# First projections of a hybrid decoder layer in pairs by seven half-sized products, and two branches' gates moved beside the RWKV chain and kept in DRAM

## The chip, the cores and the metric

The kernel runs on one core of one Trainium2 chip. The metric is the device time of one execution in microseconds, as the median of several runs. An engine here is PE (TensorE, the matrix unit), DVE (VectorE), ACT (ScalarE), POOL (GpSimd) or SP (SyncE, which issues the DMAs). Each engine executes its own program in order, and waits for semaphores that the others raise.

## What is computed

One decoder layer on x of 1024 tokens by 1024 channels, in float32. The reference, cut to what the change touches:

```python
def reference(x, mem, w_in, ...):
    p = x @ w_in[l]
    (p_rw, p_cv, g_q, g_k, g_v, g_r, g_z,
     f_q, f_k, f_v, f_z, p_gate) = _split(p, COL_SIZES)
    u_rw = _rwkv7_branch(p_rw, ...) @ rw_up[l]
    u_cv = _conv_branch(p_cv, ...) @ cv_up[l]
    u_gla = _gla_branch(g_q, g_k, g_v, g_r, g_z, ...) @ gla_up[l]
    u_fox = _fox_branch(f_q, f_k, f_v, f_z, fox_bf[l]) @ fox_up[l]
    gates = jax.nn.sigmoid(p_gate.reshape(Bsz, T, N_BRANCH, D) + gate_b[l])
    merged = (gates[:, :, 0] * u_rw + gates[:, :, 1] * u_cv
              + gates[:, :, 2] * u_gla + gates[:, :, 3] * u_fox)
    x = _layer_norm(ALPHA * x + merged @ w_out[l], ln_g[l, 0], ln_b[l, 0])
    y = _cross_attention(x, mem, xa_wq[l], xa_wk[l], xa_wv[l], xa_wo[l])
    x = _layer_norm(ALPHA * x + y, ln_g[l, 1], ln_b[l, 1])
    y = _swiglu(x, ffn_w1[l], ffn_w3[l], ffn_w2[l])
    x = _layer_norm(ALPHA * x + y, ln_g[l, 2], ln_b[l, 2])
```

`p_rw` is the input of a recurrence over the tokens (RWKV-7), which is computed in chunks; FoX is a softmax attention with a decay.

## The kernel before

All data stands transposed: channels on the 128 partitions, tokens along the free axis, in two halves `hf` of 512 tokens. w_in is cut into 57 blocks of 128 output columns: 9 for RWKV (`RW_BLOCKS`; block 8, `misc`, holds small inputs), 16 for the convolution, GLA and FoX (`ST_BLOCKS`), and 32 for the gates, 8 for each of four branches. A float32 operand is split into a rounded high part (cast on ACT) and the remainder (subtraction on DVE, sometimes POOL), by `split`; `mm3` then makes a product of three matmuls: high by high, low weights by high, high by low. A block against one half of the tokens is 8 x 3 = 24 matmuls of 128x512, so a block is 48.

The order of the work is that in which Python generators are drained, and each engine's program follows it. At first x is loaded and split into `xh`, `xl` (16 tiles of 128x1024). Then the loop over `RW_BLOCKS` (L324) projects the 9 blocks one after the other: `project` makes the matmuls into a PSUM tile `ps_g`, ACT copies them into `praw`, and five DVE operations apply the token shift (L329 to L333). Weights come by `weight` (L166): a 512 KB load into `wraw`, `whi` by ACT, `wlo` by DVE.

Then follows the chain (`rwkv`), a long row of small dependent steps. `weave` takes one piece of filler matmuls between any two steps; its filler is `stage_projections`, the 16 `ST_BLOCKS` in pieces of six matmuls, stored to DRAM. The merge comes next: `gates(br, t2)` gives, for each branch, for each of 8 row blocks j and each half, 24 gate matmuls (`ps_gate`), a sigmoid on ACT (`gsig`, L1051) and six matmuls (`ps_up`) that project the branch's output y up; DVE multiplies the two (L1056) and POOL adds them to `merged[j]` (L1057). These pieces are the filler of GLA, the convolution and FoX; of FoX's steps each takes `FOX_PIECES` of them, and what is left over is drained behind it. Then come `ps_wo` (the output projection, which reads `merged` as `mA` and `mB`), cross attention and the FFN. The FFN already pairs its blocks: the product of a 2 x 2 arrangement of quarter blocks is done by seven products of half the contraction instead of eight (a Winograd form), with combinations of weights made by `comb` and `sums` on POOL.

The loop that is replaced:

```python
    for bi, n in enumerate(RW_BLOCKS):
        raw = pM.tile([P, T], F32, tag="M", name="praw")
        drain(project(io["wblk"][bi], lambda hf, ps: nc.scalar.copy(raw[:, hs(hf)], ps),
                      (w_first, w_second, None)[min(bi, 2)]))
```

## Time and profile before

| what | value |
|---|---|
| median of 3 runs | 2102.21 us (2099.38 to 2107.37) |
| profiled execution, its own time | 2108.64 us |
| its span (first to last instruction) | 2106.9 us |
| its mean granted TensorE clock | 0.986 |
| PE busy | 2071.2 us, 98% of the span |
| DVE, ACT, POOL busy | 56%, 36%, 16% |
| projections of RW blocks; chain with ST blocks | 7 to 107 us; 107 to 447 us |
| merge with GLA and convolution; with FoX; the rest of the gates | 447 to 571.8; 571.8 to 843.5; 843.5 to 1014.2 us |

The three runs come from executions without the profiler; the trace is one further execution, whose own time stands in the second row. A busy PE means that it has matmuls in flight: they are pipelined, so the rate is read from the number of matmuls in a stretch. A granted clock of 1.00 in a window is 2.4 GHz, 0.50 is 1.2 GHz.

### The profile page before, as it was taken

The page shows a single profiled execution, that of the slowest core. Times are in us where ns is not written, and L with a number is a line of the kernel's source. Part 1 is how long each engine was busy: PE and PEld are TensorE (multiplying, and loading weights), DVE is VectorE, ACT ScalarE, POOL GpSimd, SP SyncE. Part 2 cuts the span into 40 slices and gives each one's busy share as a digit, 9 for nine tenths or more (in the row PEclk, how much of TensorE's full clock was granted, in tenths as well). Part 3 has the DMA queues.
Part 4 walks back from the last instruction along what each step waited for, and adds up shares of the span by engine and source line. Part 5 has one row for each costly group of instructions (what it writes and reads, how often), then busy time and mean ns, then how long its engine had stood idle before and what let it go on. Part 6 is the DMA issues. An engine that isn't in the chain of part 4 may idle for free.

```text
span 2106.9 us, 28921 instructions
## 1 busy us (share of the span) xinstructions
PE 2071.2 (98%) x11524; PEld 1698.4 (81%) x11524; DVE 1189.7 (56%) x2097; ACT 768.7 (36%) x1287; POOL 342.3 (16%) x268
## 2 busy tenths in 40 slices
PE   9999999999999999999999999999999999999997
PEld 7877877787888888888888888877888888888877
DVE  5465398624534443233476345677666666666666
ACT  3243222157466565222234233443232222322321
POOL 0000000000001211121024000147131111222333
PEclk9999999999999999999999999999999999999998
DMA  6123231232211211111543102331211211211102
GB/s 218 51 65 87 68 100 60 74 103 84 89 47 53 66 61 38 56 50 43 165 146 125 45 31 80 109 102 40 100 40 43 78 41 41 70 51 51 66 24 80
DMA packets 86102, 154.83 MB, mean 73 GB/s; under 512 B 19430, under 2 KB 43800, under 8 KB 85968
## 3 DMA queue, kind: packets, MB, share of 16 engines
q1 hardware_dynamic: 85968, 152.99, 22.4%
q8 instruction: 91, 1.49, 0.3%
q14 instruction: 43, 0.35, 0.1%
HBM read 128.20 MB, written 24.76 MB: 73 GB/s over the span
## 4 chain that ended last, share of the span: by engine, by line
PE 91%; DVE 2%; POOL 2%; issue 2%; ACT 1%; DMA 1%; SPq 0%; DVEq 0%; POOLq 0%; ACTq 0%
PE ps_w L183 9%; PE ps_w L179 9%; PE ps_w L182 9%; PE ps_gate L179 6%; PE ps_gate L183 5%; PE ps_gate L182 5%; PE ps_g L179 5%; PE ps_g L183 4%; PE ps_g L182 4%; PE ps_q L182 3%; PE ps_q L183 3%; PE ps_q L179 2%; PE ps_up L179 1%; PE ps_up L182 1%; PE ps_up L183 1%
## 5 line engine op out<-in xcount | busy, mean ns | idle before, releaser
L183 PE MATMUL ps_gate<-xl,whi 128*128 128x512 f32 x512 | 201.6, 394 | 0.0
L182 PE MATMUL ps_gate<-xh,wlo 128*128 128x512 f32 x512 | 201.3, 393 | 0.0
L162 DVE TENSOR_TENSOR wlo<-wraw,whi 128x1024 fp32r<-128x1024 f32 x99 | 136.5, 1379 | 61.6 <-ACT whi L161 61.4
L179 PE MATMUL ps_gate<-xh,whi 128*128 128x512 f32 x512 | 165.6, 402 | 0.0
L182 PE MATMUL ps_g<-xh,wlo 128*128 128x512 f32 x400 | 158.3, 396 | 0.0
L183 PE MATMUL ps_g<-xl,whi 128*128 128x512 f32 x400 | 158.2, 396 | 0.0
L183 PE MATMUL ps_w<-hid,piece 128*128 128x512 f32 (+1 forms) x400 | 145.4, 370 | 2.4 <-DVE hid L162 2.4
L182 PE MATMUL ps_w<-hid,piece 128*128 128x512 f32 (+1 forms) x400 | 144.8, 369 | 0.0
L161 ACT CAST whi<-wraw 128x1024 fp32r<-128x1024 f32 x117 | 122.0, 1048 | 55.9 <-issue 17.9
L179 PE MATMUL ps_g<-xh,whi 128*128 128x512 f32 x400 | 139.9, 414 | 1.7 <-ACT xh L161 1.7
L1057 POOL TENSOR_TENSOR merged<-merged,gsig 128x512 f32<-128x512 f32 x48 | 66.4, 1384 | 398.8 <-DVE gsig L1056 289.2
L161 ACT CAST piece<-wraw 128x512 fp32r<-128x512 f32 x102 | 62.4, 621 | 170.6 <-PE ps_w L183 160.7
L1593 DVE TENSOR_TENSOR x<-x,ps_w 128x512 f32<-128x512 f32 x120 | 82.4, 686 | 65.3 <-PE ps_w L183 65.1
L183 PEld LDWEIGHTS ps_gate<-xl,whi 128*128 128x128 f32 x512 | 96.9, 189 | 20.7 <-issue 0.2
L182 PEld LDWEIGHTS ps_gate<-xh,wlo 128*128 128x128 f32 x512 | 96.7, 189 | 20.6 <-issue 0.2
L182 PE MATMUL ps_w<-xT,piece 128*128 128x512 f32 x288 | 112.0, 389 | 0.0
L183 PE MATMUL ps_w<-xT,piece 128*128 128x512 f32 x288 | 112.0, 389 | 0.0
L179 PEld LDWEIGHTS ps_gate<-xh,whi 128*128 128x128 f32 x512 | 94.7, 190 | 19.3 <-issue 1.9
L179 PE MATMUL ps_w<-hid,piece 128*128 128x512 f32 (+1 forms) x400 | 110.0, 371 | 0.2 <-DVE x L1591 0.2
L1056 DVE TENSOR_TENSOR gsig<-gsig,ps_up 128x512 f32<-128x512 f32 x48 | 33.0, 687 | 132.1 <-PE ps_up L183 113.4
L162 POOL TENSOR_TENSOR wlo<-wraw,whi 128x1024 fp32r<-128x1024 f32 x18 | 46.3, 2578 | 324.6 <-ACT whi L161 249.2
L161 ACT CAST piece<-wcomb 128x512 fp32r<-128x512 f32 x72 | 43.9, 620 | 133.4 <-PE ps_w L183 132.9
(502 smaller groups left out, 4841.9 us busy)
## 6 DMA issues: line engine op xcount, KB each, us to landing
wraw<-ffn_w SPq DMA_DIRECT2D x72, 512.0 KB
wraw<-wblk SPq DMA_DIRECT2D x57, 512.0 KB
wraw<-xa_wo SPq DMA_DIRECT2D x16, 512.0 KB
xraw<-xT SPq DMA_DIRECT2D x16, 256.0 KB
yld<-y_d SPq DMA_DIRECT2D x16, 256.0 KB
uraw<-ups SPq DMA_DIRECT2D x32, 128.0 KB
wraw<-w_out SPq DMA_DIRECT2D x8, 512.0 KB
xr<-xT SPq DMA_DIRECT2D x16, 256.0 KB
```

What stands on the lines that cost most here:

```text
L161: nc.scalar.copy(hi, src)
L162: eng.tensor_tensor(out=lo, in0=src, in1=hi.bitcast(F32), op=ALU.subtract)
L179: mm(ps, lhsT=pairs[i][0], rhs=pairs[i][2], start=start and i == 0, stop=False)
L182: mm(ps, lhsT=ll, rhs=rh, start=False, stop=False)
L183: latest[0] = mm(ps, lhsT=lh, rhs=rl, start=False, stop=stop and i == n + min(lag, n) - 1)
L1056: tt(out=sg, in0=sg, in1=pu, op=ALU.mult)
L1057: nc.gpsimd.tensor_tensor(out=mj, in0=mj, in1=sg, op=ALU.add)
L1593: tt(out=xs, in0=xs, in1=ps, op=ALU.add)
```

## The change

Blocks 0, 1 and 8 are projected as before (`plain`). The other 22 first blocks, 6 of RWKV and the 16 `ST_BLOCKS`, are done in 11 pairs by `Sevens`, ahead of the chain: seven products of 12 matmuls per pair. The sevens need combinations of quarters of x (tokens' halves by halves of the contraction): three new operands, and a fourth that overwrites a quarter of `xh`, `xl`, which is loaded from DRAM and split again behind the last pair. POOL makes the four for each of four k, one of them in place of `xraw`, and ACT and DVE split them, between blocks 0, 1 and 8. POOL also combines the weights (`sums`), whose buffers are those tagged `stg`, shared with the constants `lvf` and `cef`.

The chain's filler becomes `gate_projections`: the 16 gate blocks of branches 2 and 3, evacuated by ACT's sigmoid and stored to `gate_d` in DRAM. In the merge, `gates` computes the gate of branches 0 and 1 as before; for branches 2 and 3 a piece is a load of the stored sigmoid into `gsig` (three buffers where there were two) and the six `ps_up` matmuls. `FOX_PIECES` falls from 4 to 3, and the splits of the first half of `merged` for `ps_wo` move into branch 3's gates.

```diff
-FOX_PIECES = 4
+FOX_PIECES = 3
...
-    for bi, n in enumerate(RW_BLOCKS):
...
+    class Sevens:
...
+        def product(self, rh, alloc):
+            self.top_up()
+            ps = alloc()
+            w, (h, l) = self.made[self.used], rh
+            mm3(ps, [(w[:, 0, k * P:(k + 1) * P], w[:, 1, k * P:(k + 1) * P], h[k], l[k]) for k in range(HK)])
+            self.used += 1
+            return ps
+
+        def seven(self, rhs, alloc, term, done):
+            u, v = term()
+            nc.scalar.copy(u, self.product(rhs[0], alloc))
+            done(0, 0, u, self.product(rhs[1], alloc))
+            tt(out=u, in0=u, in1=self.product(rhs[2], alloc), op=ALU.add)
+            tt(out=v, in0=u, in1=self.product(rhs[3], alloc), op=ALU.add)
+            ps = self.product(rhs[4], alloc)
+            tt(out=u, in0=u, in1=ps, op=ALU.add)
+            done(1, 1, v, ps)
+            done(1, 0, u, self.product(rhs[5], alloc))
+            done(0, 1, v, self.product(rhs[6], alloc))
...
+        plain(0, w_first)
...
+        for k in range(HK):
+            (b11, b12), (b21, b22) = ([xraw[i][:, hs(hf)] for hf in range(2)] for i in (k, k + HK))
+            t1 = comb(b12, b11, ALU.subtract)
+            split(xt[0][0][k], xt[0][1][k], t1)
+            t2 = comb(b22, t1, ALU.subtract)
+            split(xt[1][0][k], xt[1][1][k], t2)
+            t3 = comb(b22, b12, ALU.subtract)
+            split(xt[2][0][k], xt[2][1][k], t3)
+            nc.gpsimd.tensor_tensor(out=b11, in0=b21, in1=t2, op=ALU.subtract)
+        plain(1, w_second)
+        plain(8, between=lambda: sv.top_up(3))
...
+        x12 = quarter(0, 1)
+        for k in range(HK):
+            split(x12[0][k], x12[1][k], xraw[k][:, hs(0)])
+        rhs0 = (quarter(0, 0), quarter(1, 0), xt[1], xt[0], xt[2], x12, quarter(1, 1))
...
+        for b in pairs0[0:3]:
...
+            sv.seven(rhs0, bank0, term, done)
...
+        for b in pairs0[3:]:
...
+            sv.seven(rhs0, bank0, term, done)
+        for k in range(HK):
+            t = pM.tile([P, TH], F32, tag="M", name="x12")
+            nc.sync.dma_start(t, io["xT"][k][:, hs(1)])
+            split(x12[0][k], x12[1][k], t)
...
-    def stage_projections(s2):
...
+    def gate_projections(s2):
+        for i in range(16):
+            def evac(hf, ps):
                 t = s2.tile([P, TH], F32, tag="stg2", name="stg2")
...
+                act(t, ps, AF.Sigmoid, bias=pc("gateb", 16 + i))
+                nc.sync.dma_start(gate_d[i, :, hs(hf)], t)
+
+            yield from project(io["wblk"][len(BLOCKS) + 16 + i], evac, pieces=4, both=False)
...
             for hf in range(2):
...
+                sg = t2.tile([P, TH], F32, tag="sg", name="gsig", bufs=3)
+                if br < 2:
...
+                else:
+                    nc.sync.dma_start(sg, gate_d[br * 8 + j - 16, :, hs(hf)])
+                    pu = gps("ps_up", both=False)
```

Where instructions stand now, at three places.

**PE and DVE at the start.** PE's program before, from the end of block 1 (`whi_178`) into block 2 (`whi_327`, `wlo_328`):

```order
L179 MATMUL ps_g_331<-xh_112,whi_327 128x512
L179 MATMUL ps_g_331<-xh_113,whi_327 128x512
L179 MATMUL ps_g_331<-xh_114,whi_327 128x512
L182 MATMUL ps_g_331<-xh_112,wlo_328 128x512
L183 MATMUL ps_g_331<-xl_120,whi_327 128x512
L179 MATMUL ps_g_331<-xh_115,whi_327 128x512
```

and after the change, from the first matmul behind block 1; block 8's weights are `whi_408` and `wlo_409`, `piece_455` is the first weight of a pair:

```order
L179 MATMUL ps_g_412<-xh_112,whi_408 128x512
L179 MATMUL ps_g_412<-xh_113,whi_408 128x512
L179 MATMUL ps_g_412<-xh_114,whi_408 128x512
L179 MATMUL ps_g_461<-xh_112,whi_408 128x512
L179 MATMUL ps_g_461<-xh_113,whi_408 128x512
L179 MATMUL ps_g_461<-xh_114,whi_408 128x512
L179 MATMUL ps_g_528<-xh_116,piece_455 128x512
L179 MATMUL ps_g_528<-xh_117,piece_455 128x512
L179 MATMUL ps_g_528<-xh_118,piece_455 128x512
L179 MATMUL ps_g_528<-xh_119,piece_455 128x512
L182 MATMUL ps_g_412<-xh_112,wlo_409 128x512
L183 MATMUL ps_g_412<-xl_120,whi_408 128x512
```

The first matmul with a low half of new weights is the fourth of that list before and the eleventh after. DVE makes that low half. Its program before, ahead of it, has the token shift of block 0 or 1 only:

```order
L153 CAST lvl_86<-lvf_190 128x512
L329 TENSOR_SCALAR r0_197<-praw_266 128x1
L330 TENSOR_TENSOR r0_197<-praw_266 128x511
L332 SCALAR_TENSOR_TENSOR r0_197<-r0_197,par_84,praw_266 128x512
L162 TENSOR_TENSOR wlo_328<-wraw_325,whi_327 128x1024
```

After the change the low half stands behind the splits of the combinations of x, whose sources `wcomb` POOL makes:

```order
L162 TENSOR_TENSOR xt_294<-wcomb_329,xt_292 128x512
L162 TENSOR_TENSOR xt_286<-wcomb_334,xt_284 128x512
L162 TENSOR_TENSOR xt_290<-wcomb_338,xt_288 128x512
L331 SCALAR_TENSOR_TENSOR r1_198<-r1_198,par_84,praw_347 128x512
L162 TENSOR_TENSOR xt_294<-wcomb_342,xt_292 128x512
L162 TENSOR_TENSOR wlo_409<-wraw_406,whi_408 128x1024
L162 TENSOR_TENSOR piece_455<-wraw_438,piece_455 128x512
```

What moved is that `wlo` of the third block to be projected waits, by program order, for the last combination of x.

**POOL at the start.** POOL had no tensor work there before. Its first five now are these, where `wcomb_299` takes the buffer that `lvf` is cast from, and `wcomb_303` that of `cef`:

```order
L389 TENSOR_TENSOR wcomb_295<-xraw_104 128x512
L389 TENSOR_TENSOR wcomb_299<-xraw_108,wcomb_295 128x512
L389 TENSOR_TENSOR wcomb_303<-xraw_108,xraw_104 128x512
L448 TENSOR_TENSOR xraw_104<-xraw_108,wcomb_299 128x512
L389 TENSOR_TENSOR wcomb_308<-xraw_105 128x512
```

Sixteen such instructions, four for each k, stand ahead of the first combination of weights.

**SP at the end of the gates.** Before, SP there issues the loads of gate weights (`wblk`) and of the up-projections (`ups`) in turn:

```order
L166 DMA wraw_8058<-wblk 128x1024
L1032 DMA uraw_8136<-ups 128x256
L166 DMA wraw_8142<-wblk 128x1024
L1032 DMA uraw_8220<-ups 128x256
L166 DMA wraw_8226<-wblk 128x1024
L1032 DMA uraw_8304<-ups 128x256
L166 DMA wraw_8310<-wblk 128x1024
```

After the change, behind the store of FoX's last output, it is the loads of stored gates, of the branches' outputs and of the next stage's weights:

```order
L1123 DMA y_d3_2070<-fo_8262 128x512
L1210 DMA gsig_8314<-gate_d_2071 128x512
L1210 DMA gsig_8325<-gate_d_2071 128x512
L166 DMA wraw_8998<-w_out 128x1024
L1210 DMA gsig_8342<-gate_d_2071 128x512
L1184 DMA yld_8300<-y_d2_2069 128x512
L1184 DMA yld_8304<-y_d2_2069 128x512
L1190 DMA uraw_8392<-ups 128x256
L166 DMA wraw_9033<-w_out 128x1024
L166 DMA wraw_9068<-w_out 128x1024
L1184 DMA yld_8534<-y_d3_2070 128x512
L1184 DMA yld_8538<-y_d3_2070 128x512
```

A load of `gsig` waits for POOL's addition that read the tile three pieces earlier (for `gsig_8342` the last addition of branch 1), and what stands behind it in this list waits with it. On PE, behind FoX, 33 pieces of six `ps_up` matmuls follow one another, without gate matmuls between them.

## Rows read from the trace of the kernel before

**Rows 1.** The page: busy time by engine; granted clock in 40 slices; chain's shares.
```profile
PE 2071.2 (98%) x11524; PEld 1698.4 (81%) x11524; DVE 1189.7 (56%) x2097; ACT 768.7 (36%) x1287; POOL 342.3 (16%) x268
...
PEclk9999999999999999999999999999999999999998
...
PE 91%; DVE 2%; POOL 2%; issue 2%; ACT 1%; DMA 1%; SPq 0%; DVEq 0%; POOLq 0%; ACTq 0%
```

**Rows 2.** Windows by stage: busy time (x instructions) per engine, PEclk, DMA share, GB/s.
```profile
50.00:100.00 50.00, 50.00 (x222) 41.43 (x221) 19.70 (x29) 13.20 (x18) 0.44 (x2) 1.00 0.14 43
107.00:447.00 340.00, 339.91 (x2824) 264.37 (x2823) 215.77 (x455) 92.33 (x178) 8.36 (x10) 0.99 0.25 77
447.00:571.80 124.80, 123.07 (x903) 97.58 (x902) 62.34 (x154) 82.01 (x121) 3.63 (x4) 0.93 0.29 92
571.80:843.50 271.70, 271.70 (x1517) 221.20 (x1516) 115.54 (x249) 168.94 (x276) 36.23 (x27) 1.00 0.17 54
843.50:1014.20 170.70, 169.54 (x749) 140.06 (x748) 56.09 (x61) 40.83 (x63) 33.87 (x25) 1.00 0.17 52
1550.00:1600.00 50.00, 50.00 (x223) 41.40 (x222) 31.72 (x46) 15.76 (x27) 10.67 (x8) 1.00 0.22 74
```

**Rows 3.** PE's waits, one releaser: total us, times, longest us.
```profile
PE ps_v L1271 <- POOL wlo L162: 3.1, 1, 3.1
```

**Rows 4.** Timeline at the start, 20 to 31 us, three engines.
```profile
21.97 0.43 DVE L153 CAST lvl<-lvf 128x512 bf16<-128x512 f32 x1
...
22.31 0.41 ACT L157 CAST ce<-cef 128x256 fp32r<-128x256 f32 x1 [1.97 <-DMA cef<-consts]
...
27.97 1.22 DVE L162 TENSOR_TENSOR wlo<-wraw,whi 128x1024 fp32r<-128x1024 f32 x1
...
30.45 0.84 PE L179 MATMUL ps_g<-xh,whi 128*128 128x512 f32 x3
```

**Rows 5.** Groups by line and form: busy us, mean ns of one, idle before.
```profile
L161 ACT CAST piece<-wraw 128x512 fp32r<-128x512 f32 x102 | 62.4, 621 | 170.6 <-PE ps_w L183 160.7
...
L1510 POOL TENSOR_TENSOR wcomb<-wraw 128x512 f32<-128x512 f32 x38 | 49.9, 1313 | 69.8 <-DMA wraw<-ffn_w 47.0 <-DVE piece L162 21.5
...
L1510 POOL TENSOR_TENSOR wcomb<-wcomb,wraw 128x512 f32<-128x512 f32 x20 | 30.8, 1541 | 22.1 <-DVE piece L162 11.4 <-issue 6.4 <-POOL wcomb L1510 3.4
L1510 POOL TENSOR_TENSOR wcomb<-wraw,wcomb 128x512 f32<-128x512 f32 x18 | 25.6, 1420 | 312.0 <-DVE piece L162 312.0
...
L1423 POOL TENSOR_TENSOR xdiff<-x,xT 128x512 f32<-128x512 f32 x4 | 6.9, 1716 | 21.4 <-DVE xT L162 21.4
```

**Rows 6.** Windows of 2 us around 1156 us, first and last.
```profile
1156.00:1158.00 2.00, 1.68 (x8) 1.68 (x9) 2.00 (x3) 0.00 (x0) 2.00 (x2) 0.50 0.45 174
...
1160.00:1162.00 2.00, 2.00 (x10) 1.85 (x10) 1.18 (x2) 0.37 (x1) 0.00 (x0) 0.59 0.02 6
```

**Rows 7.** Timeline of two FoX steps: last score matmul, normalised probabilities.
```profile
802.29 0.23 PE L936 MATMUL ps_fs<-lvl,identb 128*128 128x128 bf16 x1
...
806.64 0.69 DVE L950 TENSOR_SCALAR fp<-fp,fst 128x896 f32<-128x896 f32 x1
...
811.48 0.23 PE L936 MATMUL ps_fs<-lvl,identb 128*128 128x128 bf16 x1
...
814.73 0.69 DVE L950 TENSOR_SCALAR fp<-fp,fst 128x896 f32<-128x896 f32 x1
```

**Rows 8.** Lines L1056 and L1057 alone: ns least/median/most, first and last start.
```profile
L1056 DVE TENSOR_TENSOR gsig<-gsig,ps_up x48: 679/687/689, 634.7 to 1012.0; 128x512 f32<-128x512 f32 x48
...
L1057 POOL TENSOR_TENSOR merged<-merged,gsig x48: 1278/1292/2208, 635.5 to 1012.8; 128x512 f32<-128x512 f32 x48
```

**Rows 9.** Timeline: two kinds of loads on SP, and a cast behind one.
```profile
19.56 0.35 SPq L156 DMA_DIRECT2D cef<-consts  x1
...
905.26 0.93 SPq L1026 DMA_DIRECT2D yld<-y_d  x2
...
908.89 1.29 ACT L161 CAST yh<-yld 128x512 fp32r<-128x512 f32 x2 [1.06 <-DMA yld<-y_d]
```

More of the change, by code (lines that the diff above doesn't have):

```diff
@@ L322, in shift_dst, with shift @@
         return rkv[n[0]][hf][:, int(n[1]), :]
-    for bi, n in enumerate(RW_BLOCKS):
-        raw = pM.tile([P, T], F32, tag="M", name="praw")
-        drain(project(io["wblk"][bi], lambda hf, ps: nc.scalar.copy(raw[:, hs(hf)], ps),
-                      (w_first, w_second, None)[min(bi, 2)]))
+    def shift(bi, raw):
+        n = RW_BLOCKS[bi]
         d0, d1 = shift_dst(n, 0), shift_dst(n, 1)
@@ new lines, in comb, with sums, plain @@
+    def comb(a, b, op):
+        t = stg.tile([P, TH], F32, tag="stg", name="wcomb")
+        nc.gpsimd.tensor_tensor(out=t, in0=a, in1=b, op=op)
+        return t
+    def sums(raws):
+        a11, a21, a22 = raws[0][:, 0:TH], raws[1][:, 0:TH], raws[1][:, TH:]
+        s1 = comb(a21, a22, ALU.add)
+        s2 = comb(s1, a11, ALU.subtract)
+        return s1, s2, comb(a11, a21, ALU.subtract)
+    def plain(bi, w=None, between=None):
+        raw = pM.tile([P, T], F32, tag="M", name="praw")
+        g = project(io["wblk"][bi], lambda hf, ps: nc.scalar.copy(raw[:, hs(hf)], ps), w)
+        drain(g, 1)
+        if between:
+            between()
+        drain(g)
+        shift(bi, raw)
@@ L701, in hybrid_kernel @@
         ps1 = es.enter_context(tc.tile_pool(name="ps1", bufs=4, space=PSUM))
[L702 removed]
+        rwkv(t1, ps1, gate_projections(s2))
     def log_sigmoid(dst, x, tmp):
@@ L1013, in conv, with __init__ @@
         ready.add(1)
-    merged = []
+    merged, mh = [], []
+    class HL:
+        def __init__(self, pool, tag, name, n=KD):
+            self.h, self.l = [], []
+            for lst in (self.h, self.l):
+                for _ in range(n // 2):
+                    t = pool.tile([P, 2, TH], F32R, tag=tag, name=name)
+                    lst += [t[:, 0], t[:, 1]]
     def gates(br, t2):
@@ L1058, in gates @@
                 yield
+            if br == 3:
+                if not mh:
+                    mh.append(HL(pB, "B", "mA"))
+                if j:
+                    split(mh[0].h[j - 1], mh[0].l[j - 1], merged[j - 1][:, hs(0)])
     def merge(t2):
@@ L1506, in rows @@
         return raws
-    def comb(a, b, op):
-        t = stg.tile([P, TH], F32, tag="stg", name="wcomb")
-        nc.gpsimd.tensor_tensor(out=t, in0=a, in1=b, op=op)
-        return t
     pairs_f = list(range(LEAD, NFF, 2))
```

131 lines of the change are left out of this document (84 added, 47 removed).

## Prediction

> **What bounds the kernel now.** I read the page first: PE is busy 98% of the span and holds 91% of the chain of work that ended last, at a granted clock of nine tenths or more in all slices but the last, which is at eight [rows 1]. So a PE instruction that goes away is worth its time, wherever the others keep up, and a new PE wait costs its full length. The windows then show what the others have to spare stage by stage [rows 2]. In the stretch of plain first projections (50 to 100 us) 222 matmuls of 128x512 fit into 50 us, 0.2252 us each. In the FFN, which already uses seven products per pair, it is 223 in 50 us, with DVE at 31.7 us of 50, ACT at 15.8 and POOL at 10.7: that scheme feeds PE at full rate here. The chain (107 to 447), FoX (571.8 to 843.5) and the rest of the gates behind it (843.5 to 1014.2) leave PE idle 0.1, 0 and 1.2 us. The reader should see that PE is saturated in every stretch that the change touches; the question is what saves PE time, and where the change lets PE run dry.
>
> **The change part by part, against the profiled execution** (2108.64 us, with a span of 2106.9 and 1.7 us around it; 6.4 us above the median of 2102.21, so the sum's difference is carried over to the median).
>
> *Removed.* Eleven pairs of blocks take 7 products of 12 matmuls, 84, instead of 2 x 48 = 96: 132 matmuls fewer, at 0.2252 us [rows 2], **-29.7 us**. The 768 gate matmuls that move into the chain cost the same wherever they stand. If waits took it all back the gain would be 0; more than 29.7 it can't be, as no other PE work goes.
>
> *The start.* POOL now makes 16 combinations of x, and DVE and ACT split 12 of them, while PE does blocks 0 and 1. The second combination takes the buffer of `lvf` and needs its cast, which ended at 21.97 + 0.43 = 22.4 us; the third takes that of `cef`, cast until 22.72 [rows 4]. So POOL starts its remaining 15 at 22.4. Nearest durations for the same shape: 1.31, 1.42 and 1.54 us by whether an operand is fresh, and 1.72 where DVE works beside it; the least is 1.28 [rows 5, 8]. I take 1.45, since most wait for the one before: 15 x 1.45 = 21.8, end 44.2 (41.6 to 48.2). Behind that stand the ACT cast of 0.62 [rows 5], the DVE subtraction of 0.69 (the shape of the 687 ns row, [rows 8]) and, in DVE's program order behind it, `wlo_409`, the low half of block 8's weights, 1.22 us [rows 4]. With 0.2 for the hand-overs it is ready at 46.9. PE comes out of block 1 at 30.45 [rows 4] and has ten matmuls, 2.3 us, that need no low half; it then waits for `wlo_409` from 32.7 to 46.9, **+14.2 us** (11.6 to 18.2). Before, the same place found its weights' low half at 27.97 + 1.22 = 29.2, ahead of PE. Queued behind this wait on PE is everything; on DVE and ACT the pieces of the first pair then come during the 42 other matmuls of block 8 (9.5 us), so I put no second wait. The other DMA issues of the start stand ahead of those loads as before.
>
> *Clock after that wait.* A wait of 3.1 us on PE [rows 3] was followed by 0.50 of the granted clock, which is 1.2 GHz, at 1156 to 1158 and still 0.59 at 1160 to 1162 [rows 6]. About 5.6 us of such time lose half, **+2.8** (0 to 3.5).
>
> *Steady sevens.* As in the FFN [rows 2], with one DVE evacuation more per product for token shift: **+1** (0 to 5). The quarter of x that is overwritten comes back by four loads at the end; two products, 24 matmuls or 5.4 us, lie behind the moment at which its buffer is free, and they hide it; without them it would be one load and split, within those 5 us.
>
> *The chain.* Its filler is 768 matmuls as before, in the same pieces, evacuated by a sigmoid instead of a copy. PE idled 0.1 us there [rows 2], and the chain's steps are tied to PE's pieces, so **0**; at most 10, if the sigmoid's table switches make the chain itself late in each of its sixteen blocks by 0.6, about the length of an ACT pass [rows 5].
>
> *FoX with three pieces between steps.* From the last score matmul to the normalised probabilities it was 802.29 to 807.33, 5.0 us, in one step and 811.48 to 815.42, 3.9 us, in the next [rows 7]; the first had an ACT table switch in it. Four pieces of six matmuls cover 24 x 0.2252 = 5.4 us, three cover 4.05. In the 16 steps without attention products in between, half with the switch miss 0.95: 8 x 0.95 = 7.6 at most by this pattern and 15 if all do; the other 16 have those products as cover. I take **+5** (0 to 15).
>
> *The end of the gates.* Before, 749 matmuls were left there, with 48 gate matmuls ahead of each use of a sigmoid tile [rows 2]. Now 33 pieces of six `ps_up` matmuls follow each other, which PE could do in 33 x 6 x 0.2252 = 44.6 us (47.3 with the last 12 gate matmuls ahead of them), 1.35 each. But each needs its sigmoid tile loaded into one of three buffers, and that load waits on SP for POOL's addition three pieces earlier. One turn is: landing, DVE multiply 0.69, POOL addition 1.29 [rows 8], hand-overs 0.25. No load of a single 256 KB tile is shown; a pair of them went from issue at 905.26 to the cast's start at 908.89, 3.6 us; a tile of 128 KB (`cef`) took from 19.56 to 22.31, 2.75 [rows 4, 9]. I take 3.2, between the two. That is 5.45 per turn of three pieces, 1.8 us a piece (1.66 to 1.95), above PE's 1.35. The first turn is later still: behind the third tile's load, which waits for branch 1's last addition (6.2 us into this stretch: 12 + 6 matmuls, 4.1, then 0.69 and 1.29), SP holds the second half of branch 2's `y`; landing, casts and the multiply put the fourth tile's landing at about 18 us. Then 28 more pieces by 1.8 = 50.4, so the last multiply comes at 68.4, and `ps_wo`, which needs the last addition of the first half, starts then: 68.4 - 47.3 = **+21**; I take **+20** (12 to 26), as the last piece or two are not needed by the first `ps_wo`.
>
> A sentence that the sum doesn't need: the Trainium skill ("DMA: Bandwidth & Descriptors", Anatomy of one DMA) puts a transfer on GpSimd's path at some 2.0 us fixed plus bytes over 436 GB/s, which makes an estimated 2.6 us for this tile; these loads are issued by SP, and by that page the end would cost about 15 and the total come to 2110. The trace does not show this transfer; the nearest rows, 2.75 and 3.6 [rows 4, 9], both lie above the page's figure.
>
> Sum: -29.7 + 14.2 + 2.8 + 1 + 0 + 5 + 20 = **+13.3**: 2121.9 for an execution like the profiled one, **2115.5 against the median**.
>
> **Rivals.**
> (B) The same waits at their low ends: POOL at 1.28 (11.6), three pieces enough, landing 2.75 (a piece 1.66, end +14): -29.7 + 11.6 + 2.8 + 1 + 14 = 0, **2102**. For it: POOL's least times are real. Against it: its means are above [rows 5].
> (C) The end of the gates is hidden: not slower. If a turn of load, multiply and add is below three pieces of PE, 4.05 us, PE never waits there. That needs a landing under 4.05 - 0.69 - 1.29 - 0.25 = 1.8 us. Without the +20 the sum is -6.7, **2095.5**, and 2087 with the start and FoX at low ends. Against it: no row shows a landing that short [rows 4, 9]. For it: those rows contain casts that may have come late for other reasons.
> (D) The clock stays down. In the end of the gates PE is busy three quarters of the time, in the start it stands 14 us. At 1.2 GHz a piece takes 2.7 us, more than the turn: 33 x 2.7 = 89 in place of 68, **2135**. For it: 0.50 after a wait of 3.1 us [rows 3, 6]. Against it: the clock came back within 6 us there.
> That the change does not do what it says (PE work not removed) is out: the count of PE instructions falls from 10046 to 9914, by those 132.
>
> **How the numbers follow.** Forecast 0.48, B 0.15, C 0.21, D 0.16. The range reaches from 2090 to 2134: within C to its middle, and up to D; the forecast's own is 2106 to 2126. A measurement tells about 0.5% (10.5 us: 2091.7 to 2112.7) from no change. Faster: half of C and a little of what I don't see, 0.15. Same: B, the other half of C and the forecast's low quarter, 0.37. Slower: 0.48.
>
> **What would show it.** The start: PE idle about 14 us from near 33, released by DVE's `wlo`, with POOL busy in `wcomb` from 22 to 44. The sevens: 222 matmuls in 50 us up to the chain, which begins some 30 - 17 = 13 us earlier than 107. FoX: PE waits for DVE's `fp` under 1 us each. The end: `ps_up` pieces 1.8 us apart, SP waiting for POOL's `merged`, and 68 us between the last gate matmul's neighbourhood and `ps_wo`. It is wrong if the 33 pieces run at 1.35 us, or if POOL's combinations start well before 22 us, or if DVE has `wlo_409` before them.

## The result, and the profile after

The changed kernel took 2136.44 us (median of 4 runs, 2130.96 to 2137.93) against 2104.79 for the kernel before beside it: a ratio of 1.0149, interval 1.0119 to 1.0179, **32 us slower**. The direction is as forecast; the time lies 2 us above the range. The profiled execution took 2136.71 us with a span of 2134.9, 28 us above the span of before.

The page after, busy time by engine and the shares of the chain that ended last; it answers to [rows 1]:

```profile
PE 2056.8 (96%) x11392; PEld 1677.5 (79%) x11392; DVE 1300.1 (61%) x2249; ACT 784.8 (37%) x1334; POOL 435.2 (20%) x328
...
PE 84%; DVE 4%; POOL 3%; DMA 3%; ACT 3%; issue 2%; SPq 0%; DVEq 0%; POOLq 0%; ACTq 0%
```

132 PE instructions are gone (11524 to 11392), as the change says, but PE's busy time fell by 14 us only, and its share of the chain from 91% to 84%: work of DVE, POOL, ACT and DMAs now sets the end in places. The waits of PE say which (total us, times, longest):

```profile
PE ps_up L179 <- DVE gsig L1218: 11.7, 9, 2.5
PE ps_g L182 <- DVE wlo L162: 11.5, 1, 11.5
PE ps_up L179 <- ACT yh L161: 9.7, 3, 3.8
PE ps_g L179 <- ACT whi L161: 5.5, 1, 5.5
```

Before, only the third was there, once, with 1.2 us. Windows of after (the start; steady sevens; the chain; the merge up to FoX's last product; the rest of the gates), with the columns of [rows 2]:

```profile
30.40:62.00 31.60, 14.60 (x47) 11.05 (x46) 25.15 (x24) 10.78 (x19) 20.47 (x14) 0.68 0.14 50
...
62.00:273.60 211.60, 211.60 (x934) 175.00 (x933) 140.74 (x194) 61.88 (x103) 64.56 (x49) 1.00 0.28 90
...
273.60:616.30 342.70, 341.24 (x2819) 264.96 (x2819) 214.56 (x455) 107.26 (x191) 8.80 (x12) 0.99 0.28 87
616.30:957.20 340.90, 338.41 (x2176) 270.67 (x2174) 162.78 (x383) 221.70 (x363) 27.15 (x23) 0.98 0.21 64
957.20:1040.50 83.30, 59.77 (x213) 43.23 (x212) 51.09 (x67) 22.13 (x38) 45.89 (x31) 0.88 0.60 192
```

and of before for the last two, cut at the same matmuls (FoX's last product ends at 842.8 there, the first `ps_wo` starts at 1011.7):

```profile
447.10:842.80 395.70, 393.97 (x2415) 318.13 (x2413) 177.89 (x402) 250.39 (x396) 39.86 (x31) 0.98 0.21 66
...
842.80:1011.70 168.90, 167.74 (x741) 138.57 (x739) 55.41 (x60) 40.69 (x62) 32.58 (x24) 1.00 0.16 50
```

Two stretches stand out, the first and the last: PE busy 14.60 of 31.60 and 59.77 of 83.30, at clocks of 0.68 and 0.88. The account, each stretch against its matmuls at 0.2252 us (a window's count includes up to three that reach over its bounds):

| stretch | forecast | measured |
|---|---|---|
| matmuls removed, 132 x 0.2252 | -29.7 | -29.7 |
| start, its clock, sevens: first chain matmul 165.5 us later, 143.2 of it the 636 matmuls now ahead of it | +18.0 | +22.3 |
| chain, 342.7 against 339.0 before | 0 | +3.7 |
| merge up to FoX's last product, 340.9 against 395.7, with 240 matmuls fewer (54.0) | +5 | -0.8 |
| end of the gates, 83.3 against 210 x 0.2252 = 47.3 | +20 | +36.0 |
| what the kernel before lost in its own end of the gates, 168.9 against 738 x 0.2252 = 166.2 | 0 | -2.7 |
| sum | +13.3 | +28.8 |

The sum is that of the two profiled executions, where the first `ps_wo` starts at 1040.5 instead of 1011.7. The profiled execution of before took 4 us more than its median, so the medians lie 32 apart.

PE's timeline at the start (start, duration, instruction, idle before and releaser):

```profile
36.13 2.93 PE L179 MATMUL ps_g<-xh,whi 128*128 128x512 f32 x6 [5.50 <-ACT whi L161]
38.85 1.91 PE L179 MATMUL ps_g<-xh,piece 128*128 128x512 f32 x4
52.26 0.79 PE L182 MATMUL ps_g<-xh,wlo 128*128 128x512 f32 x1 [11.50 <-DVE wlo L162]
```

The ten matmuls between the waits take 4.6 us where full speed makes 2.25, and those from 52.26 on follow each other by 0.43 until 55.8: beside the 17.0 of waits some 4 go to the clock. What PE waited for, on POOL, on ACT and on DVE:

```profile
23.02 1.28 POOL L389 TENSOR_TENSOR wcomb<-xraw,wcomb 128x512 f32<-128x512 f32 x1 [8.92 <-DVE lvl L153]
...
47.55 1.71 POOL L389 TENSOR_TENSOR wcomb<-xraw 128x512 f32<-128x512 f32 x1
```

```profile
34.02 0.62 ACT L161 CAST xt<-wcomb 128x512 fp32r<-128x512 f32 x1 [2.72 <-POOL wcomb L389]
...
35.03 1.05 ACT L161 CAST whi<-wraw 128x1024 fp32r<-128x1024 f32 x1
```

```profile
29.43 1.77 DVE L329 TENSOR_TENSOR r<-praw 128x512 f32<-128x512 f32 x1
...
50.39 0.68 DVE L162 TENSOR_TENSOR xt<-wcomb,xt 128x512 fp32r<-128x512 f32 x1
50.99 1.21 DVE L162 TENSOR_TENSOR wlo<-wraw,whi 128x1024 fp32r<-128x1024 f32 x1
```

POOL began near the forecast 22.4 and ended at 49.26 instead of 44.2; `wlo` ended at 52.2 instead of 46.9. ACT made `whi` only at 35.03, in its order behind the cast of a combination that POOL finished at 34.0. DVE's operations took up to 1.77 us while POOL worked and 0.68 once it had stopped.

In the end of the gates, branch 3's part of the timeline, all engines:

```profile
1025.59 2.72 POOL L1219 TENSOR_TENSOR merged<-merged,gsig 128x512 f32<-128x512 f32 x2 [1.29 <-DVE gsig L1218]
...
1027.57 1.29 DVE L162 TENSOR_TENSOR mA<-merged,mA 128x512 fp32r<-128x512 f32 x1 [0.40 <-ACT mA L161]
...
1028.78 0.67 DVE L1218 TENSOR_TENSOR gsig<-gsig,ps_up 128x512 f32<-128x512 f32 x1
...
1029.60 2.72 POOL L1219 TENSOR_TENSOR merged<-merged,gsig 128x512 f32<-128x512 f32 x2 [1.29 <-DVE gsig L1218]
1029.60 0.70 PE L179 MATMUL ps_up<-yh,uh 128*128 128x512 f32 x2 [1.04 <-DVE gsig L1218]
...
1029.99 0.69 DVE L1218 TENSOR_TENSOR gsig<-gsig,ps_up 128x512 f32<-128x512 f32 x1 [0.54 <-DMA gsig<-gate_d]
```

Two pieces take 4.01 us (1025.59 to 1029.60), 2.0 each where 1.8 was forecast. The load behind the first of the two additions (ended 1026.9) releases a multiply at 1029.99: a turn's landing is 3.1 us (I took 3.2). New is that DVE stands, in its order, at a split of `mA` ahead of the next multiply, waiting for POOL and ACT. Between branch 2 and branch 3 stands something longer, the change from one `y` to the other. DVE's multiply for the fourth stored tile, for the last of branch 2, the first of branch 3 and the last of all, and a cast on ACT in the change:

```profile
977.15 0.69 DVE L1218 TENSOR_TENSOR gsig<-gsig,ps_up 128x512 f32<-128x512 f32 x1
...
1004.13 0.69 DVE L1218 TENSOR_TENSOR gsig<-gsig,ps_up 128x512 f32<-128x512 f32 x1 [0.27 <-DMA gsig<-gate_d]
...
1011.74 0.69 DVE L1218 TENSOR_TENSOR gsig<-gsig,ps_up 128x512 f32<-128x512 f32 x1 [1.93 <-PE ps_up L183]
...
1041.79 0.69 DVE L1218 TENSOR_TENSOR gsig<-gsig,ps_up 128x512 f32<-128x512 f32 x1 [0.48 <-DMA gsig<-gate_d]
```

```profile
1008.47 0.62 ACT L161 CAST yh<-yld 128x512 fp32r<-128x512 f32 x1 [4.52 <-DMA yld<-y_d]
```

The change takes 7.6 us (1004.13 to 1011.74), and the cast that PE waits for waits itself for a load of `y`. The clock was at 0.50 behind such waits (968 to 974 and 1009 to 1015) and at 0.57 from 994 to 998; elsewhere it was 1.00, also where PE waited about 1 us every 4:

```profile
968.00:974.00 6.00, 5.15 (x12) 4.08 (x13) 3.69 (x5) 3.48 (x5) 1.79 (x1) 0.50 0.81 292
...
1015.00:1040.00 25.00, 19.67 (x80) 14.40 (x80) 19.90 (x26) 5.87 (x12) 17.71 (x13) 1.00 0.46 148
```

### The profile page after: what moved, and what is told of

It reads as the page before. It is cut to its first block, busy times and chain, and to the rows that moved or that the text cites. A ratio compares the mean times of both kernels' runs of the same rounds, so it can differ in the third digit from the quotient of the medians.

```text
span 2134.9 us, 29251 instructions
## 1 busy us (share of the span) xinstructions
PE 2056.8 (96%) x11392; PEld 1677.5 (79%) x11392; DVE 1300.1 (61%) x2249; ACT 784.8 (37%) x1334; POOL 435.2 (20%) x328
## 3 DMA queue, kind: packets, MB, share of 16 engines
q8 instruction: 90, 1.47, 0.3%
## 4 chain that ended last, share of the span: by engine, by line
PE 84%; DVE 4%; POOL 3%; DMA 3%; ACT 3%; issue 2%; SPq 0%; DVEq 0%; POOLq 0%; ACTq 0%
PE ps_w L183 9%; PE ps_w L182 9%; PE ps_w L179 9%; PE ps_g L179 7%; PE ps_g L183 6%; PE ps_g L182 6%; PE ps_q L182 3%; PE ps_q L183 3%; PE ps_q L179 2%; PE ps_gate L179 2%; PE ps_gate L183 2%; PE ps_gate L182 2%; PE ps_wo L183 1%; PE ps_wo L182 1%; PE ps_wo L179 1%
## 5 line engine op out<-in xcount | busy, mean ns | idle before, releaser
L182 PE MATMUL ps_g<-xh,wlo 128*128 128x512 f32 x304 | 121.2, 399 | 11.5 <-DVE wlo L162 11.5
L162 DVE TENSOR_TENSOR wlo<-wraw,whi 128x1024 fp32r<-128x1024 f32 x77 | 98.3, 1278 | 53.4 <-ACT whi L161 53.2
L389 POOL TENSOR_TENSOR wcomb<-wraw,wcomb 128x512 f32<-128x512 f32 x29 | 41.4, 1429 | 401.6 <-DVE piece L162 400.6
L183 PE MATMUL ps_g<-xl,whi 128*128 128x512 f32 x304 | 121.5, 400 | 0.0
L162 DVE TENSOR_TENSOR piece<-wraw,piece 128x512 fp32r<-128x512 f32 x127 | 97.4, 769 | 35.1 <-ACT piece L161 32.6
L389 POOL TENSOR_TENSOR wcomb<-wraw 128x512 f32<-128x512 f32 x60 | 83.0, 1384 | 108.3 <-DVE piece L162 52.1
L183 PE MATMUL ps_gate<-xl,whi 128*128 128x512 f32 x256 | 101.6, 397 | 0.0
L182 PE MATMUL ps_gate<-xh,wlo 128*128 128x512 f32 x256 | 100.7, 394 | 0.0
L162 DVE TENSOR_TENSOR piece<-wcomb,piece 128x512 fp32r<-128x512 f32 x116 | 91.3, 794 | 11.6 <-ACT piece L161 10.8
L183 PEld LDWEIGHTS ps_w<-hid,piece 128*128 128x128 f32 x400 | 77.7, 194 | 14.7 <-DVE hid L162 2.7
```

Source lines behind the costliest of these rows:

```text
L162: eng.tensor_tensor(out=lo, in0=src, in1=hi.bitcast(F32), op=ALU.subtract)
L182: mm(ps, lhsT=ll, rhs=rh, start=False, stop=False)
L183: latest[0] = mm(ps, lhsT=lh, rhs=rl, start=False, stop=stop and i == n + min(lag, n) - 1)
L389: nc.gpsimd.tensor_tensor(out=t, in0=a, in1=b, op=op)
```

## The experiments

Each edit is against the changed kernel; each ratio against the kernel before, run beside it on the same chip (2103.8 to 2105.9). Differences in us are to 2136.4, which was not run again beside them, so a difference of 3 us says little. The theory: the start loses by DVE's place for `wlo` behind POOL's combinations, the end by the turn of the stored tiles. Rivals: the loads alone; the change of y; the contention of DVE and POOL.

### The end of the gates

**tail_16_tiles**: the stored sigmoids go into a tile of both halves from a larger pool, so that their loads wait for nothing.

```diff
+                if br < 2:
+                    sg = t2.tile([P, TH], F32, tag="sg", name="gsig", bufs=3)
+                else:
+                    if hf == 0:
+                        sgt = pA.tile([P, T], F32, tag="A", name="gsig")
+                    sg = sgt[:, hs(hf)]
```

> The stored gates of branches 2 and 3 are loaded into sixteen tiles, those of xh and xl, which are free by then, instead of three; all else is the changed kernel. Theory (a load waits for POOL's addition three pieces earlier, and PE for that turn): the stretch from FoX's last product to the first output projection falls from 83 us to 55 to 65, and the whole to about 2113 (2105 to 2120). Rival 1 (the transfers themselves are what is slow there, beside the w_out loads): the stretch stays at 78 to 85, the whole at 2131 to 2138. Rival 2 (POOL's additions at 1.3 to 1.4 us set the pace): 33 additions fill 45 us, so the stretch is 55 to 60 too, but PE then waits for POOL's pace to the end and the additions follow each other without gaps.

2127.45, 1.0106 [1.0085, 1.0128]: -9, not -23. The loads are out of the turn; what they had hidden remains, PE's waits at the end:

```profile
PE ps_up L179 <- ACT yh L161: 9.7, 3, 5.0
PE ps_up L179 <- DVE gsig L1223: 7.5, 7, 1.4
```

The change of y is unchanged at 9.7: `yh` and `yl` have one set of buffers, so the first half of the next `y` is cast only when the last product with the one before is done. `yld` has two buffers, so the second half is loaded only behind that cast, and 9.5 of the 9.7 end with casts that waited for this load:

```profile
968.26 0.62 ACT L161 CAST yh<-yld 128x512 fp32r<-128x512 f32 x1 [4.53 <-DMA yld<-y_d]
```

And branch 2's pieces then run at POOL's pace, 1.47 each, above PE's 1.35; two of branch 3's still take 4.1 to 4.7. Branch 2's on POOL:

```profile
981.37 14.70 POOL L1224 TENSOR_TENSOR merged<-merged,gsig 128x512 f32<-128x512 f32 x10 [0.20 <-POOL merged L1224]
```

**tail_dve_add**: the addition of branches 2 and 3 on DVE instead of POOL, loads as in the change.

```diff
-                    nc.gpsimd.tensor_tensor(out=mj, in0=mj, in1=sg, op=ALU.add)
+                    (nc.vector if br >= 2 else nc.gpsimd).tensor_tensor(out=mj, in0=mj, in1=sg, op=ALU.add)
```

> The additions of branches 2 and 3 go from POOL to DVE; three tiles as in the changed kernel. Theory: a turn loses 0.6 to 0.7 us of its 6 (landing, multiply, addition), so the 33 pieces gain 33 x 0.2 = 7 us and the whole is about 2129 (2125 to 2133). Rival (POOL's pace is what limits): each piece falls to DVE's pace and PE's 1.36, the stretch by 20 us or more, the whole to 2115. Rival (transfers): under 3 us.

2123.67, 1.0089 [1.0068, 1.0111]: -12.8, more than the 7 of the theory's shorter turn and less than the 21 of its rival. Groups of DVE's operations in the last 80 us of the gates, of after:

```profile
L162 DVE TENSOR_TENSOR ul<-uraw,uh 128x256 fp32r<-128x256 f32 x15 | 10.1, 675 | 1.3 <-ACT uh L161 1.3
L162 DVE TENSOR_TENSOR mA<-merged,mA 128x512 fp32r<-128x512 f32 x7 | 8.7, 1239 | 2.9 <-ACT mA L161 2.9
```

and of this run:

```profile
L162 DVE TENSOR_TENSOR ul<-uraw,uh 128x256 fp32r<-128x256 f32 x15 | 6.2, 420 | 0.2 <-ACT uh L161 0.2
L162 DVE TENSOR_TENSOR mA<-merged,mA 128x512 fp32r<-128x512 f32 x8 | 5.5, 688 | 0.2
```

With POOL still, the same splits take 420 and 688 ns instead of 675 and 1239. So DVE does the additions and has time left. How much of the 12.8 is the shorter turn and how much the splits isn't separated.

**tail_16_late_splits**: tail_16_tiles, with the splits of `mA` written behind branch 3's pieces.

```diff
...
-                if j:
-                    split(mh[0].h[j - 1], mh[0].l[j - 1], merged[j - 1][:, hs(0)])
...
-        for j in range(0 if hf else KD - 1, KD):
+        for j in range(KD):
```

> As tail_16_tiles, and the splits of merged for the output projection are taken out of branch 3's pieces again and follow all of them, as in the kernel before. With sixteen tiles the loads no longer limit, yet branch 3's sixteen pieces still took 4.0 to 4.7 us per two. Theory A: there DVE, in order, stands at the split of the row before, which needs POOL's addition and ACT's cast of it, and the multiply behind it holds the PSUM bank that PE waits for; without the splits two pieces take 2.7 to 3.2 us, the stretch falls by 8 to 12 us, and the whole by 5 to 10 against tail_16_tiles (2127), since some of the splits come later. Theory B: DVE's slower work beside POOL's is the bound by its sum; then the splits cost as much behind the pieces, and the whole stays within 3 us of 2127.

2126.26, 1.0096 [1.0073, 1.0119]; 1.2 from tail_16_tiles, nothing. The test failed as a test: on DVE the splits still stood between the multiplies (one at 1004.03, between those at 1003.10 and 1005.73). What they cost alone stays open.

**branch_order_0213**: stored branch 2 ahead of branch 1, so that its pieces run in FoX and branch 1's, with gate matmuls, end the gates with branch 3's.

```diff
-        for br in range(4):
+        for br in (0, 2, 1, 3):
```

> The changed kernel with branch 2, whose gates are stored, merged before branch 1, whose gates are computed: the pieces left behind FoX are then about 17 of branch 1, with gate matmuls, and 16 of branch 3, instead of 33 without gate matmuls. Theory (the loss behind FoX is that of pieces without gate matmuls, in load turns, switches of y and a low clock): half of them go, so half of 36 us: the whole falls by 14 to 20, to about 2119 (2115 to 2124). Rival (branch 2's load turns then stall FoX, whose own loads queue behind them on SP): FoX takes 8 us or more longer, and the whole stays above 2126.

2129.54, 1.0114 [1.0096, 1.0132]: -7, below the -14 to -20 expected, and both numbers of the rival came true. The end lost 17 us instead of 36, but the stored pieces lose in FoX too; a window there:

```profile
800.00:820.00 20.00, 14.32 (x55) 10.78 (x53) 12.05 (x25) 9.52 (x21) 3.97 (x3) 0.83 0.42 131
```

PE is busy 14.3 of 20 us at a clock of 0.83; FoX lasts 232.0 us against 221.2. The rival's reason, FoX's own loads, is not what PE waits for: in this window it waits 5.7 us for `yh`, the change to branch 2's y, and the matmuls behind it follow by 0.43. It is not the place in the program that loses, but stored pieces in a row, which cover no change of y.

**fox_four_pieces**: `FOX_PIECES = 4`, as before the change.

> The changed kernel with FOX_PIECES back at 4, nothing else. More pieces go into FoX, so fewer of those without gate matmuls are left behind it: about 40 to 60 more pieces are taken up, and the stretch behind FoX falls to little. Theory (the loss is that of pieces without gate matmuls run back to back): what is taken up lies between FoX's own matmuls, and the whole falls by 12 to 25. My forecast of a gain from four pieces by FoX's own waits is not tested by it, since the trace shows none of those waits. Rival: the loaded pieces stall FoX instead, by the load turns and by y switches, and the sum stays within 5 us of 2136.

2142.12, 1.0161 [1.0131, 1.0191]: +5.7 in the median, with intervals that overlap, where the theory had -12 to -25. With four, branch 2's stored pieces run inside FoX, and at its end nothing is left to cover its steps, as branch 3 needs FoX's own output: in the last 96 us up to its end PE waits 6.7 for `yh`, 4.7 for `gsig`, 5.4 for `fp`. A miss: I had counted pieces, and not that these are poor cover.

**stored_rows_spread**: 16 gate blocks are stored again, but from three branches, so that at most three stored blocks follow each other and each branch begins with a full one.

```diff
+    STORED = ([(b, j) for b in (1, 2) for j in (1, 2, 4, 5, 7)] + [(3, j) for j in (1, 2, 3, 5, 6, 7)])
...
-            if br < 2:
+            if (br, j) not in STORED:
```

> The same number of gate blocks, sixteen, is computed beside the chain and stored, but as single rows j of branches 1, 2 and 3 (five, five and six of eight) instead of all of branches 2 and 3; each branch begins with a computed row. Pieces, matmuls and transfers are the same in number. Theory (the 36 us behind FoX are lost because stored pieces run back to back: their turn is longer than their six matmuls, nothing covers the change of y, and the clock falls in those waits): computed rows between them cover the turns and the change of y, the stretch's loss falls to 5 to 12 us, the whole to about 2110 (2105 to 2116). Rival (loaded pieces cost what they cost, by DVE's and POOL's work, wherever they stand): the loss is spread over the merge, and the whole stays above 2125.

2113.51, 1.0047 [1.0033, 1.0062]: **-23**, as expected. The stretch behind FoX, and FoX itself in this run and in after:

```profile
962.50:1017.10 54.60, 49.12 (x212) 39.15 (x211) 34.25 (x42) 17.88 (x29) 23.08 (x17) 1.00 0.43 134
```

```profile
735.70:962.50 226.80, 221.88 (x1286) 177.25 (x1284) 120.67 (x255) 133.29 (x243) 43.91 (x33) 1.00 0.24 75
```

```profile
736.00:957.20 221.20, 220.45 (x1287) 177.60 (x1286) 103.07 (x232) 140.53 (x243) 23.52 (x19) 1.00 0.16 47
```

The 210 matmuls take 54.6 us at full clock, where after takes 83.3: the loss there falls from 36 to 7, with as many blocks through DRAM, on the same buffers, and no wait for `yh`. FoX, with the same number of matmuls, takes 5.6 more, so the rival, a loss spread over the merge, holds for a fifth of the 29; 23 remain.

### The start

**start_w8_first**: block 8's weights are asked for behind block 0, ahead of the combinations.

```diff
+        w_eight = weight(io["wblk"][8])
...
         for k in range(HK):
...
-        plain(8, between=lambda: sv.top_up(3))
+        plain(8, w_eight, between=lambda: sv.top_up(3))
```

> Block 8's weights are asked for, and split, ahead of the combinations of x instead of behind them. Theory (program order of one low half behind the combinations costs the wait): the two waits of 5.5 and 11.5 us go, PE comes out of block 8 at 42 and then waits about 7 to 10 us for the first combined weight, since POOL's combinations still start at 23 us; the chain starts 8 to 12 us earlier than at 273.6, the whole is about 2127 (2123 to 2130). Rival (POOL and DVE slow each other so much that their work is the bound, whatever the order): the wait only moves behind block 8, the chain starts within 3 us of 273.6, the whole stays at 2133 to 2138.

2129.4, 1.0118 [1.0093, 1.0144]: -7; the first chain matmul comes 4.3 us earlier, between the theory's 8 to 12 and the rival's 3. DVE begins `wlo` at 34.95 instead of 50.99, and of the waits of 5.5 and 11.5 us one of 2.5 is left, but the gain is small: PE meets the next item of the same queue, its waits on the first weights of a pair:

```profile
PE ps_g L179 <- ACT piece L161: 5.3, 1, 5.3
PE ps_g L182 <- DVE piece L162: 2.5, 1, 2.5
PE ps_g L182 <- DVE wlo L162: 2.5, 1, 2.5
```

**start_own_const_buffers**: `lvf` and `cef` in buffers of their own, so that POOL starts early.

```diff
-        lv = stg.tile([P, TH], F32, tag="stg", name="lvf")
+        lv = pB.tile([P, T], F32, tag="B", name="lvf")[:, 0:TH]
...
-        cf = stg.tile([P, 256], F32, tag="stg", name="cef")
+        cf = pB.tile([P, T], F32, tag="B", name="cef")[:, 0:256]
```

> The two constants lvf and cef get buffers of their own kind instead of two of the three that the combinations use, so POOL needn't wait for their casts. Theory: POOL's second combination starts at 14 to 16 us instead of 23, everything behind it 7 to 9 us earlier, the chain starts at 264 to 267 instead of 273.6, the whole is about 2128 (2124 to 2131). Rival (their mutual slowing is the bound): the work starts earlier but then runs beside the splits of x, which DVE does up to 20 us, is slowed and slows them, and under 4 us are gained.

2133.47, 1.0137 [1.0114, 1.016]. POOL starts its second combination at 14.6 instead of 23.0, and the first chain matmul comes 4.9 us earlier; 3 us in the median, with intervals that overlap. The rival's mechanism: DVE is slowed while it still splits x, and PE waits there. Up to 70 us PE now waits 6.0 for `wlo`, 3.7 for `xh` and 1.4 for `xl`; the groups of DVE from 8 to 34 us, of after and of this run:

```profile
L162 DVE TENSOR_TENSOR xl<-xraw,xh 128x512 fp32r<-128x512 f32 x15 | 10.7, 754 | 0.2
```

```profile
L162 DVE TENSOR_TENSOR xl<-xraw,xh 128x512 fp32r<-128x512 f32 x15 | 17.3, 1182 | 0.2 <-ACT xh L161 0.2
```

The same 15 splits of x take 1182 ns each instead of 754.

**start_cover**: four combinations at a time, between blocks 0, 1, 2, 3 and 8, with blocks 2 and 3 projected in the plain way, weights asked for ahead. It has 12 matmuls more.

```diff
-        pairs0 = list(range(2, 8, 2)) + list(range(9, 9 + len(ST_BLOCKS), 2))
+        pairs0 = list(range(4, 8, 2)) + list(range(9, 9 + len(ST_BLOCKS), 2))
...
+        w_two = weight(io["wblk"][2])
+        x_terms(0)
         plain(1, w_second)
+        w_three = weight(io["wblk"][3])
+        x_terms(1)
+        plain(2, w_two)
...
```

> One pair fewer by sevens: blocks 2 and 3 are projected plainly, which adds 12 matmuls, 2.7 us, and the combinations of x are spread between the five plain blocks, each block's weights asked for ahead of them. Theory (the start's loss of 22 us is want of cover for POOL's 25 us of combinations and their splits): PE's waits there fall from 17 us to under 4, the clock stays up, and the whole falls by 14 to 19, to about 2120 (2116 to 2124). Rival (the work of DVE and POOL, which slow each other, is the bound in the start whatever PE does meanwhile): the five plain blocks add DVE work too, 6 us, and less than 8 us are gained.

2123.98, 1.0083 [1.0064, 1.0102]: -12.5, a little below the 14 to 19 expected, with the first chain matmul at 261.4 instead of 273.6. One wait is left from 20 to 70 us, 4.4 us for `wlo`.

**start_combos_on_dve**: the 16 combinations of x on DVE instead of POOL.

```diff
-            t1 = comb(b12, b11, ALU.subtract)
+            t1 = comb_v(b12, b11, ALU.subtract)
...
```

> The sixteen combinations of x go from POOL to DVE; nothing else in the changed kernel. Theory (DVE's subtractions of two SBUF tensors take 1.4 to 1.8 us instead of 0.69 while POOL runs one of its own, and POOL's 1.7 instead of 1.29): DVE alone does 16 combinations, 12 splits and both token shifts in about 28 us from 21, so they end near 49 as before, although DVE has 11 us more to do; the chain starts within 3 us of 273.6 and the whole is 2132 to 2139. Rival (no slowing of one by the other; DVE is simply long): the combinations add 16 x 0.69 = 11 us to what DVE does by 51, PE waits 11 us longer, and the whole is 2145 to 2150.

2125.63, 1.0099 [1.0082, 1.0115]: -11 (`comb_v` is `comb` on `nc.vector`), and I had expected 2132 to 2139, since it gives 11 us of work to the engine that stands last. Groups of DVE at the start (20 to 60 us), of after and of this run:

```profile
L162 DVE TENSOR_TENSOR xt<-wcomb,xt 128x512 fp32r<-128x512 f32 x12 | 15.6, 1324 | 2.2 <-ACT xt L161 2.1
```

```profile
L162 DVE TENSOR_TENSOR xt<-wcomb,xt 128x512 fp32r<-128x512 f32 x12 | 8.1, 686 | 6.3 <-ACT xt L161 6.3
L442 DVE TENSOR_TENSOR wcomb<-xraw 128x512 f32<-128x512 f32 x8 | 5.5, 682 | 0.0
```

Alone, DVE does a combination in 0.68 (POOL took up to 1.74) and its own splits in half the time. But `wlo` also moved ahead, to 26.95, in the built program, so order and contention were mixed. Hence the next.

**w8_first_combos_on_dve**: start_w8_first and start_combos_on_dve together, so that block 8's low half stands ahead of most splits in both.

> start_w8_first with the combinations of x on DVE; in both, block 8's low half stands ahead of most splits, so its place in the order is no longer in question. start_combos_on_dve had gained 11 us, but there the low half also moved ahead. Theory A (that gain was the low half's place): start_w8_first, which has it ahead too, gained 7 us, so only 4 more are left for DVE; the chain starts at 263 to 267. Theory B (the gain is that POOL no longer slows DVE): DVE's operations take 0.69 instead of up to 1.77 us, its last split of x ends at 46 to 48 instead of 54, and the chain starts at 258 to 262.

2122.42, 1.009 [1.0076, 1.0105]: -7 beside start_w8_first, the first chain matmul 7.7 us earlier (261.6). The last split of the combinations on DVE, in start_w8_first and here:

```profile
52.49 1.77 DVE L162 TENSOR_TENSOR xt<-wcomb,xt 128x512 fp32r<-128x512 f32 x1
```

```profile
48.55 0.70 DVE L162 TENSOR_TENSOR xt<-wcomb,xt 128x512 fp32r<-128x512 f32 x1 [2.32 <-ACT xt L161]
```

It ends 5 us earlier, with 16 operations more on DVE. The 7 us are what moving the combinations gains, and three things are in them that this pair doesn't separate: DVE's operations take 0.7 instead of up to 1.8, a combination takes 0.68 on DVE where POOL's fastest took 1.28, and `wlo` came earlier still, at 26.6 (PE waited 2.5 for it in start_w8_first, and not here). (I had said 46 to 48 for the end of the splits; it was 49.25, behind ACT.)

### Together

**spread_and_cover** (stored_rows_spread and start_cover):

> stored_rows_spread and start_cover together. Theory (the two losses are apart in time and independent): the gains add, 12 and 26 us off 2136, so about 2098 (2092 to 2104), which is faster than the kernel before by 0.1 to 0.6%. Rival: the gains don't add, and the whole stays above 2108.

2101.96, 0.9988 [0.9978, 0.9998]: the two gains add.

**spread_cover_consts** (that with own buffers for the constants):

> As spread_and_cover, with buffers of their own for the two constants, as in start_own_const_buffers. Theory: PE's remaining wait of 4.4 us for a low half at 35 us goes, as POOL starts earlier, and 2 to 5 us are gained on spread_and_cover: about 2094 (2089 to 2100). Rival: POOL's earlier work slows the splits of x themselves, as it did there, and nothing is gained (within 2 us of spread_and_cover, or above).

2108.8, 1.0025 [1.0012, 1.0037], 7 us worse: again POOL runs into the splits of x (PE waits for `xh` 4.1, `wlo` 3.8, `xl` 1.5, against 1.6, 2.4 and none). A miss.

**spread_combos_on_dve** (stored_rows_spread and start_combos_on_dve):

> stored_rows_spread with the combinations of x on DVE. The two changed places are 650 us apart, so the gains of 23 and 11 us should add: 2136.4 - 23 - 11 = about 2102.5 (2098 to 2107). Rival: they don't add; above 2109.

2101.95, 0.9981 [0.9969, 0.9993]: adds too.

**spread_cover_combos_on_dve** (all three):

> spread_and_cover with the combinations of x on DVE. In spread_and_cover PE still waits 2.4 us for a low half and about 1 us at 60 to 80 us, and POOL still slows DVE. Theory: those waits go, 2 to 5 us are gained on 2102: 2097 to 2100, the fastest of all. Rival (with five plain blocks DVE has no room for 11 us more before 50 us): a wait for the last combinations takes its place, and the whole is 2102 to 2107.

**2094.89, 0.9959 [0.9947, 0.9972]**: the fastest, 2 us below the range expected, 41.5 below the change and 9.9 below the kernel before. Its start and its end:

```profile
20.00:60.00 40.00, 40.00 (x178) 33.12 (x177) 36.66 (x55) 16.42 (x28) 6.13 (x3) 1.00 0.29 92
946.00:1000.00 54.00, 49.01 (x224) 39.31 (x219) 33.64 (x41) 18.67 (x30) 22.65 (x17) 1.00 0.40 130
```

PE has no idle time from 20 to 60 us; the first chain matmul comes at 256.5, 17 us earlier than in the change, with 12 matmuls (2.7 us) more ahead of it.

## Why the prediction was right or wrong

**Removed, sevens: right.** 132 matmuls went (the prediction counts PE's instructions as 10046 and 9914, the page as 11524 and 11392); from 62 to 273.6, 934 took 211.6 us, 1.3 above 934 x 0.2252 (+1 forecast). No wait stands there. One sign was wrong, without a part in the sum: the chain doesn't begin 13 us earlier than 107, but at 273.6, since all 11 pairs stand ahead of it.

**Start: the mechanism was right, the size 4 us short.** The wait is where it was put and ends with `wlo`. The step that failed is "I take 1.45" for a combination. The rows of POOL alone (1.28 to 1.54) were taken, though the one beside DVE, 1.72, was read; here 13 of the 15 took 1.59 to 1.74, with 1.9 us of waits between them, 1.2 of it for one of DVE's splits. Nor is it a fresh operand that sets the 1.42 and 1.54 apart: in the trace of before each of the three forms takes 1.28 to 1.31 in all 27 cases where DVE does no operation on two SBUF operands beside it, and up to 1.8 only beside one. The steps behind POOL held: cast, subtraction (0.68) and `wlo` took 2.9 us from its end where 2.7 were forecast. I had also put one wait; there were two, as ACT, in order at the cast of a combination, made `whi` late by 5.5. The clock term, 2.8, became about 4, because two waits lower it.

**Chain: 0 forecast, +3.7.** One wait of 1.4 "issue" and a stretch from 285 to 290 at 0.50 are part of it; the rest is unexplained.

**FoX: +5 forecast, +1.5.** It takes 221.2 us, 49.6 less than before, with 227 matmuls (51.1) fewer. The waits for `fp` total 0.4 us. Three pieces covered its steps; the 5.0 us of one step pair in [rows 7] didn't recur as a loss. Nor is it an ACT table switch that sets that step apart: the trace of before has one in each of the two, at 803.58 and at 811.16. The merge ahead of FoX gained 2.3, at a clock of 0.96 where before had 0.93; why it was higher is open. fox_four_pieces shows what three buy: work that is left for behind FoX.

**End of the gates: the mechanism was part of it, +20 became +36.** This is the larger error. The step that failed is "28 more pieces by 1.8 = 50.4". The piece with the fourth tile came 20 us into the stretch, near the 18 forecast for its landing; the last one came 64.6 later. Of the 28, one stands behind the change to branch 3's y, 7.6 us after the piece before it, and the sum has nothing for that (it has the change to branch 2's y, in the first turn). The other 27 took 2.1 each. The landing was right, 3.1 against 3.2; an addition took 1.26 to 2.29 instead of 1.29, and DVE stood at splits of `mA`.

Told by PE, 23.4 of the 36 are waits (11.7 for `gsig`, 9.7 for `yh`, 2.0 for `uh`). Some 7.5 more go to some 30 matmuls that follow each other by 0.43, 24 of them behind waits for `yh`: the clock, which I had priced for the start alone. The other 5 stand at the first and last matmuls beside the waits. So the two changes of y, with the slow matmuls behind them, are about 15 of the 36, the largest part. Without the turn 9 us go (tail_16_tiles), without POOL's additions 12.8 (tail_dve_add). These overlap, so a full division isn't settled; stored_rows_spread takes 29 at once and gives 6 back in FoX.

The estimate of 2.6 us for a tile, worked out from a figure that the Trainium skill (DMA: Bandwidth & Descriptors, "Anatomy of one DMA") states for GpSimd's path, is below the 3.1 measured for these loads on SP.

**Rivals.** B fell, with POOL above 1.59 in 13 of 15 and a landing of 3.1. C needed a landing under 1.8 us and fell at 3.1. D is the nearest in time by luck: its own terms give 2115.5 + 89 - 68 = 2136.5, not the 2135 written, and 2136.4 was measured. But the clock was at or near 0.50 for some 20 of the 83 us, not throughout, and cost 7.5 of the 36.
